# ReLU and row sum over 64 MB: own semaphores, multi-row instructions and a split memory layout

## Chip, cores, metric

The kernel runs on one core of one Trainium2 chip and uses no other. The metric is the device time of one execution in microseconds (us). Every run also has a traced span, from the first to the last instruction of the program. All runs quoted are marked fast in the record (none is more than 1.5% above the fastest of its kernel), with a granted clock of 1.0.

## The reference

```python
batch, seq, dim = 32, 512, 1024
x = np.random.randn(batch, seq, dim).astype(np.float32)

def reference(x):
    relu_x = np.maximum(x, 0)
    return np.sum(relu_x, axis=-1).astype(np.float32)
```

That is 16384 rows of 4 KB: 67.1 MB to read, 64 KB to write, hardly any arithmetic.

## The kernel before

Each of the 128 partitions owns 128 consecutive rows, so the 128 read streams of a load are 512 KB apart in memory. Seven loads of 16 rows per partition (8 MB each) go through two buffers; then come 8, 4, 2 and 1 rows and the last row in four pieces. Every row is one call that does ReLU and sum together (the profile shows two instructions for it, the second reads the accumulator), even rows on ScalarE and odd rows on VectorE.

```python
xv = x_flat.rearrange("(p m) d -> p (m d)", p=P)
out2d = out.rearrange("b s -> (b s)").rearrange("(p m) -> p m", p=P)
chunks = [16] * 7 + [8, 4, 2, 1]
io_pool = ctx.enter_context(tc.tile_pool(name="io", bufs=2))
...
for j, cpd in enumerate(chunks):
    xt = io_pool.tile([P, cpd, D], fp32, ...)
    nc.sync.dma_start(out=xt, in_=xv[:, m0 * D : (m0 + cpd) * D]...)
    for c in range(cpd):
        m = m0 + c
        if m == NT - 2:
            act_op(...)
            nc.scalar.dma_start(out=out2d[:, 0 : NT - 2], in_=res[:, 0 : NT - 2])
        elif (c % 2) == 0:
            act_op(xt[:, c, :], xt[:, c, :], m)       # ReLU with accumulated sum
        else:
            dve_op(xt[:, c, :], xt[:, c, :], res[:, m : m + 1])
    m0 += cpd
# last row in pieces of 244, 252, 260, 268 columns, all on VectorE; then:
nc.sync.dma_start(out=out2d[:, NT - 2 : NT], in_=res[:, NT - 2 : NT])
```

The first load is issued ahead of the program's opening barrier, in both kernels.

## Time and profile before

| | before |
|---|---|
| time, median (range) | 163.64 us (163.27 to 163.69), 3 runs |
| traced span | 161.5 us |
| load queue's packets, share of 16 engines | 96.9% |
| VectorE, ScalarE busy | 46%, 43% |

The page of the kernel before: the engines' busy time, the DMA queues (packets, MB, share of 16 engines), and the two costliest groups (busy us, mean ns of one | idle us before them, and what ended it):

```profile
DVE 74.3 (46%) x134; ACT 69.0 (43%) x129; POOL 0.2 (0%) x4
...
q1 hardware_dynamic: 2304, 67.11, 96.9%
q10 hardware_dynamic: 144, 0.06, 0.1%
q14 instruction: 2, 0.02, 0.0%
...
L79 DVE TENSOR_SCALAR_CACHE_REDUCE xt<-xt 128x1024 f32<-128x1024 f32 x63 | 72.6, 1216 | 84.5 <-DMA xt<-in_x_dram 84.2
L71 ACT ACTIVATE xt<-xt 128x1024 f32<-128x1024 f32 x64 | 66.7, 1043 | 89.0 <-DMA xt<-in_x_dram 89.0
```

Both compute engines are idle more than half of the time, waiting for loads. The line `q14` is easily passed over: two packets, together 16 KB, with which the engines' instruction streams are refilled, on the same 16 DMA engines as the loads.

The timeline of VectorE shows where each block of 16 rows has landed (start us, duration us, instruction, and in brackets the idle time before it; only the first instruction of a block is kept):

```profile
22.27 1.22 DVE L79 TENSOR_SCALAR_CACHE_REDUCE xt<-xt 128x1024 f32<-128x1024 f32 x1 [22.27 <-DMA xt<-in_x_dram]
...
61.08 1.22 DVE L79 TENSOR_SCALAR_CACHE_REDUCE xt<-xt 128x1024 f32<-128x1024 f32 x1 [10.27 <-DMA xt<-in_x_dram]
80.43 1.22 DVE L79 TENSOR_SCALAR_CACHE_REDUCE xt<-xt 128x1024 f32<-128x1024 f32 x1 [10.14 <-DMA xt<-in_x_dram]
100.27 1.22 DVE L79 TENSOR_SCALAR_CACHE_REDUCE xt<-xt 128x1024 f32<-128x1024 f32 x1 [10.63 <-DMA xt<-in_x_dram]
119.62 1.22 DVE L79 TENSOR_SCALAR_CACHE_REDUCE xt<-xt 128x1024 f32<-128x1024 f32 x1 [10.15 <-DMA xt<-in_x_dram]
```

The gaps are 19.35 us, but from 80.43 to 100.27 it is 19.84. The packet records and the landing events (semaphore updates by a DMA engine) in the trace say why. They are not a view of the page, so here they are in a plain fence:

```
instruction packets of 8192 bytes within the span: at 86.35 and 86.65 us, 309 ns each
last two of a block's 16 landing events:   block 3   80.20, 80.29 us
                                           block 4   99.63, 100.13 us
```

From block 4 on one engine is about half a microsecond behind the other fifteen, and a block has landed when its last engine has. The delay stays to the end. The ordinary 64 KB packet takes 2418 ns, so 16 engines carry 16 x 65536 B / 2.418 us = 433.7 GB/s. The Trainium skill's fabric ceiling is 435 GB/s ("DMA: Bandwidth & Descriptors", Where 436 GB/s comes from); the trace agrees. The same passage lets about 358 GB/s bind for loads from HBM; the loads of this one core run above that.

### The profile page before, as it was taken

The numbers are of one execution on the slowest core, as the hardware profiler recorded it, in microseconds if no ns is written. First come the engines' busy times: TensorE is split into PE (matmuls) and PEld (weight loads), VectorE is DVE, ScalarE is ACT, GpSimd is POOL, SyncE is SP. The second block draws the span as 40 slices with busy tenths as digits, with TensorE's granted clock in tenths as the row PEclk, the third lists the DMA queues.
The fourth block names the chain that finished last, engine by engine and source line by source line (L and its number), as shares of the span: only waits on it lengthen the run. The fifth ranks groups of instructions, "written<-read, shape, count | busy, mean of one in ns | idle before, by whom it ended". The sixth has DMA issues, their size and how long they took to land.

```text
span 161.5 us, 347 instructions
## 1 busy us (share of the span) xinstructions
DVE 74.3 (46%) x134; ACT 69.0 (43%) x129; POOL 0.2 (0%) x4
## 2 busy tenths in 40 slices
DVE  0000049700695008940099101991039900598983
ACT  3000049500693008920099001990039700596882
POOL 0000000000000000000000000000000000000000
DMA  8997997996997997997996997997997997999990
GB/s 308 471 503 308 487 487 308 503 503 292 503 503 308 487 503 325 471 519 308 471 519 296 487 503 325 471 503 341 454 503 341 454 503 308 430 438 406 406 359 22
DMA packets 2450, 67.19 MB, mean 416 GB/s; under 512 B 528, under 2 KB 1040, under 8 KB 1168
## 3 DMA queue, kind: packets, MB, share of 16 engines
q1 hardware_dynamic: 2304, 67.11, 96.9%
q10 hardware_dynamic: 144, 0.06, 0.1%
q14 instruction: 2, 0.02, 0.0%
HBM read 67.11 MB, written 0.07 MB: 416 GB/s over the span
## 4 chain that ended last, share of the span: by engine, by line
DMA 79%; DVE 18%; SPq 1%; issue 0%; DVEq 0%
DMA xt<-in_x_dram 62%; DVE xt L79 17%; DMA p<-in_x_dram 17%; SPq L95 1%; DVE p L79 1%; DVEq L79 0%; DVEq L16 0%
## 5 line engine op out<-in xcount | busy, mean ns | idle before, releaser
L79 DVE TENSOR_SCALAR_CACHE_REDUCE xt<-xt 128x1024 f32<-128x1024 f32 x63 | 72.6, 1216 | 84.5 <-DMA xt<-in_x_dram 84.2
L71 ACT ACTIVATE xt<-xt 128x1024 f32<-128x1024 f32 x64 | 66.7, 1043 | 89.0 <-DMA xt<-in_x_dram 89.0
L71 ACT ACTIVATION_READ_ACCUMULATOR xt<-xt 128x1 f32 x64 | 11.9, 187 | 0.0
L79 DVE DVE_READ_ACCUMULATOR xt<-xt 128x1 f32 x63 | 5.2, 83 | 0.0
L79 DVE TENSOR_SCALAR_CACHE_REDUCE p<-p 128x244 f32<-128x244 f32 (+3 forms) x4 | 1.6, 420 | 0.4 <-DMA p<-in_x_dram 0.4
L71 ACT ACT_TABLE_LOAD x1 | 1.3, 1283 | 0.8 <-PEq L143 0.8
L79 DVE DVE_READ_ACCUMULATOR p<-p 128x1 f32 x4 | 0.3, 82 | 0.0
L143 POOL MEMSET const-bfloat16-1.0<- 128x1 bf16 x1 | 0.1, 101 | 0.0
L143 POOL MEMSET const-uint8-127<- 128x1 uint8 x1 | 0.1, 101 | 0.0
L143 POOL MEMSET const-float32-0.0<- 128x1 f32 x1 | 0.1, 98 | 0.2 <-issue 0.2
L143 POOL MEMSET const-float32-1.0<- 128x1 f32 x1 | 0.1, 98 | 0.0
## 6 DMA issues: line engine op xcount, KB each, us to landing
xt<-in_x_dram SPq DMA_DIRECT2D x1, 4096.0 KB, 19.6
xt<-in_x_dram SPq DMA_DIRECT2D x1, 2048.0 KB, 24.2
xt<-in_x_dram SPq DMA_DIRECT2D x1, 1024.0 KB, 26.2
xt<-in_x_dram SPq DMA_DIRECT2D x1, 512.0 KB, 27.0
p<-in_x_dram SPq DMA_DIRECT2D x1, 134.0 KB, 10.0
p<-in_x_dram SPq DMA_DIRECT2D x1, 130.0 KB, 26.5
p<-in_x_dram SPq DMA_DIRECT2D x1, 126.0 KB, 26.7
p<-in_x_dram SPq DMA_DIRECT2D x1, 122.0 KB, 26.8
```

The costliest lines, as they stand in the source:

```text
L71: nc.scalar.activation(out=out_ap, in_=in_ap, func=mybir.ActivationFunctionType.Relu, accum_out=res[:, m : m + 1],)
L79: nc.vector.tensor_scalar(out=out_ap, in0=in_ap, scalar1=0.0, scalar2=None, op0=mybir.AluOpType.max, op1=mybir.AluOpType.add, accum_out=ac ...
L95: nc.sync.dma_start(out=xt, in_=xv[:, m0 * D : (m0 + cpd) * D].rearrange("p (c d) -> p c d", c=cpd),)
L143: nc = _bacc.Bacc("TRN2", target_bir_lowering=False, num_devices=1)
```

## The change

Its intent: semaphores of its own in place of the framework's (one per load, so that no issue waits for a semaphore's reuse); one ReLU over up to 16 rows on ScalarE and one sum over the same rows on VectorE, so far fewer instructions; three buffers, because the two steps take longer from end to end; the first 8 MB of memory as the first block (partitions 64 KB apart), the rest as a second region (448 KB apart); all stores on SyncE, one more because the output too is now in two regions. Cut to its core:

```diff
+ROWS = 16
+NBUF = 3
+TWO = [[16], [16], [16], [8, 8], [8, 8], [6, 5], []]   # rows per ReLU and per sum
+ACT = [0, 0, 0, 0, 0, 5, 8]                             # single rows, ScalarE
+DVE = [0, 0, 0, 0, 0, 0, 8]                             # single rows, VectorE
...
-    xv = x_flat.rearrange("(p m) d -> p (m d)", p=P)
+    N1 = P * ROWS
+    xf = x_flat[:N1].rearrange("(p m) d -> p m d", p=P)
+    xv = x_flat[N1:].rearrange("(p m) d -> p m d", p=P)
...
+    def clamp(ap, loaded):                # ReLU of n rows, in place
+        i = nc.scalar.activation(out=ap, in_=ap, func=RELU)
...
+    def total(ap, m, n):                  # their sums
+        nc.vector.tensor_reduce(
+            out=res[:, m : m + n], in_=ap, axis=mybir.AxisListType.X, op=ADD
+        ).wait_op(sems.act, n_act, "sem-ge").then_inc(sems.dve, 1)
...
+    for j in range(NB):
+        buf = bufs[j % NBUF]
+        loaded = load(buf[:, :, :], rows(m, ROWS), j >= NBUF and freed[j - NBUF])
...
+        for n in TWO[j]:
+            clamp(buf[:, c : c + n, :], act_waits)
+            total(buf[:, c : c + n, :], m + c, n)
...
-                nc.scalar.dma_start(out=out2d[:, 0 : NT - 2], in_=res[:, 0 : NT - 2])
+    store(0, ROWS, *freed[0])
+    store(ROWS, NT - ROWS - 2, n_act - 1, n_dve)
...
-    nc.sync.dma_start(out=out2d[:, NT - 2 : NT], in_=res[:, NT - 2 : NT])
+    store(NT - 2, 2, n_act, n_dve)
```

The tail loads (8, 4, 2, 1 rows and four pieces) keep their sizes and their single-row instructions.

## The prediction

> **What bounds it now.** The load queue. Block landings (the timeline, where VectorE resumes) come every 19.35 us: 22.27, 41.61, 61.08, 80.43, 100.27, 119.62, 138.97; one gap is 19.84. In the trace's packet records nearly all 896 packets of 64 KB take 2418 ns, 27.1 GB/s an engine, 433.7 over 16: the ceiling of 435 that the Trainium skill gives ("DMA: Bandwidth & Descriptors", Where 436 GB/s comes from), and this trace agrees. ScalarE and VectorE wait 89.0 and 84.2 us for loads (the groups); the next load always queues 10 us before the one under way ends, so two buffers never starve the queue.
>
> Outside the stream: first packets start between 1.02 and 2.27 us, engine after engine, and take 2.55 to 3.2 us instead of 2.42; the last piece lands at 158.60; VectorE ends 159.19, the store's issue starts 159.25, it lands 160.67, the program ends 161.52.
>
> **What the change does.**
> 1. Fewer instructions. At 86.35 us, when ScalarE and VectorE have each recorded about 64 instructions, two 8 KB instruction-fetch packets (309 ns each) run on a load engine; from the next block on, one engine lands 0.49 us behind the others (100.13 against 99.63), and keeps that to the end (158.60 against 158.12). By count from the code both engines now stay below 60, so the fetches should vanish: -0.5 us, on the path.
> 2. Layout. The skill (same page, Latency and other measured facts) has a 512 KiB row pitch at 207 GB/s against 214 padded, for copies between HBM tensors. Here the 512 KB pitch already streams at full rate, so a 448 KB pitch gains nothing in mid-stream. It may cure the slow first packets: the engine that starts last loses 0.13 us there, only that counts. A few packets near 11 us are slow too, on engines with slack. -0.1 us.
> 3. Three buffers and two-pass compute. Estimated from traced slopes (ACTIVATE 1043 ns a row with about 190 fixed; VectorE 435-407 ns for 271-244 elements): ReLU of 16 rows 13.9 us, sum 17.1 us, both below 19.35. A buffer frees about 31 us after landing and the load into it goes out about 8 us before the queue empties, so still no starvation. The two engines become much busier (VectorE from 74 to about 100 us), off the path. The split [8,8], [6,5]+5 lets VectorE catch up at about 138, when block 6 lands.
> 4. Own semaphores. Two waits and a drain after the final store's landing (160.69 to 160.85) become one: -0.1 us. The wait of the third piece's issue on a reused semaphore (16.4 us, the queue's waits) goes, but it was hidden.
> 5. A third store, 64 B per partition: it queues behind the last piece and lands before the final store. About 0. The last sums and the 1.4 us of the final store remain.
>
> **Sum.** -0.5 -0.1 -0.1: about -0.7 of 163.64.
>
> Predicted 162.9 us, 162.4 to 163.4. Chances: faster by over 2% 0.01, within 2% 0.97, slower 0.02. The stream alone takes 64 x 2.418 = 154.8 us an engine, so 2% (3.3 us) can't be found in what is left.
>
> **What would show it.** No instruction packets between 0 and the end; every landing gap 19.35 us; last piece at about 158.0; span about 160.8; ACTIVATE of 128x16384 near 13.8 us and the reduction near 17.1 us; each load issued about 8 us before its predecessor lands.
>
> **What would make it wrong.** The reduction running well below one element a cycle, so that buffers come free late and the load queue runs dry (slower by several us); the 448 KB pitch or multi-row accesses slowing the 2418 ns packets; an instruction fetch moved into the tail rather than removed; the HBM's slow first packets costing more than the last engine shows, which would gain more.

## The result

| | before | changed |
|---|---|---|
| time, median (range) | 163.50 us (163.27 to 163.69), 4 runs | 163.09 us (162.92 to 163.43), 4 runs |
| ratio, 95% interval | | 0.9978 (0.9956 to 1.0001) |
| traced span of the profiled run | 161.5 us | 160.7 us |
| measured time of that run | 163.31 us | 163.14 us |
| rest (time less span) | 1.8 us | 2.4 us |

This first interval still includes 1; that of the repeat below (changed_again) doesn't.

The time lies inside the predicted range, but the traced span fell by 0.8 us and the time by 0.4: about half of the traced gain does not arrive. First the profile after, the same parts of the page:

```profile
DVE 117.0 (73%) x47; ACT 102.8 (64%) x52; POOL 0.2 (0%) x4
...
q1 hardware_dynamic: 2592, 67.18, 97.6%
...
L119 DVE TENSOR_REDUCE res<-io 128x8 f32<-128x8192 f32 (+3 forms) x9 | 97.9, 10933 | 40.1 <-ACT io L111 40.1
L111 ACT ACTIVATE io<-io 128x8192 f32<-128x8192 f32 (+3 forms) x9 | 79.2, 8826 | 47.2 <-DMA io<-in_x_dram 47.2
```

VectorE went from 46% to 73% busy and the kernel became no slower: the extra work lies under the loads. The `q14` line is gone, and the packets' share of the engines rose from 96.9% to 97.6%. The timeline of ScalarE, where the blocks land now:

```profile
21.95 13.86 ACT L111 ACTIVATE io<-io 128x16384 f32<-128x16384 f32 x1 [19.88 <-DMA io<-in_x_dram]
41.29 13.86 ACT L111 ACTIVATE io<-io 128x16384 f32<-128x16384 f32 x1 [5.48 <-DMA io<-in_x_dram]
...
80.00 13.95 ACT L111 ACTIVATE io<-io 128x8192 f32<-128x8192 f32 x2 [5.50 <-DMA io<-in_x_dram]
99.34 13.95 ACT L111 ACTIVATE io<-io 128x8192 f32<-128x8192 f32 x2 [5.39 <-DMA io<-in_x_dram]
118.70 9.68 ACT L111 ACTIVATE io<-io 128x6144 f32<-128x6144 f32 x2 [5.41 <-DMA io<-in_x_dram]
```

The first block lands 0.3 us earlier, the gap from 80.00 to 99.34 is an ordinary 19.34, and ReLU over 16 rows takes 13.86 us. The Trainium skill gives 186 ns + 0.833 ns an element for an ACTIVATE with immediate scale and bias ("ScalarE: Activation LUTs", What ACT_TABLE_LOAD costs), by which I estimate 13.83 us for 16384 elements; the trace agrees.

The chain of work that ended last, by line (shares of the span), of the kernel before:

```profile
by line: DMA xt<-in_x_dram 61.9%; DVE xt L79 17.1%; DMA p<-in_x_dram 16.6%; SPq L95 1.1%; DVE p L79 1.0%; issue 0.4%; DVEq L79 0.1%; DVEq L16 0.0%
```

The same view of the changed kernel, with two of the chain's pieces in order of time (start us, us, what):

```profile
by line: DVE res L119 32.1%; DMA io<-in_x_dram 25.2%; DMA piece<-in_x_dram 17.9%; ACT io L111 17.3%; another core or an unknown queue 3.4%; SPq L93 1.0%; DVE piece L136 0.7%; DVE piece L204 0.3%; issue 0.2%; DVEq L29 0.0%
...
74.54 51.60 DVE res L119 x5
...
126.16 0.33 SPq L93
```

This view misleads here. Loads fell from 79% of the chain to 43%, as if VectorE were the limit. The chain goes through the wait of the tail's first load for its buffer, which VectorE frees at 126.14 us; but the block before it in the queue lands only at 138.06 us, so the engines had 12 us of queued work when that issue went out. A chain follows what released an issue, not what kept the queue full. That the landing gaps stayed at 19.35 us is the better evidence.

What the page cannot show lies behind the span. The packet record of the changed kernel has one more instruction packet:

```
changed kernel:  8192 bytes of instructions at 162.81 us, 568 ns;  span ends at 160.70 us
kernel before:   none behind the span (161.52 us)
```

So the theory to test: the instruction fetch was not removed but moved behind the program's end, and there it costs what it had cost in the stream. Rivals: the layout made the whole gain; or the rest grew for another reason, such as the number of semaphores, or by chance.

### The profile page after: what moved, and what is told of

It reads as the page before. It is cut to its first block, busy times and chain, and to the rows that moved or that the text cites. A ratio compares the mean times of both kernels' runs of the same rounds, so it can differ in the third digit from the quotient of the medians.

```text
span 160.7 us, 162 instructions
## 1 busy us (share of the span) xinstructions
DVE 117.0 (73%) x47; ACT 102.8 (64%) x52; POOL 0.2 (0%) x4
## 3 DMA queue, kind: packets, MB, share of 16 engines
q1 hardware_dynamic: 2592, 67.18, 97.6%
## 4 chain that ended last, share of the span: by engine, by line
DMA 43%; DVE 33%; ACT 17%; another core or an unknown queue 3%; SPq 1%; issue 0%; DVEq 0%
DVE res L119 32%; DMA io<-in_x_dram 25%; DMA piece<-in_x_dram 18%; ACT io L111 17%; SPq L93 1%; DVE piece L136 1%; DVE piece L204 0%; DVEq L29 0%
## 5 line engine op out<-in xcount | busy, mean ns | idle before, releaser
L119 DVE TENSOR_REDUCE res<-io 128x8 f32<-128x8192 f32 (+3 forms) x9 | 97.9, 10933 | 40.1 <-ACT io L111 40.1
L111 ACT ACTIVATE io<-io 128x8192 f32<-128x8192 f32 (+3 forms) x9 | 79.2, 8826 | 47.2 <-DMA io<-in_x_dram 47.2
L126 ACT ACTIVATE io<-io 128x1024 f32<-128x1024 f32 x21 | 21.9, 1044 | 6.8 <-DMA io<-in_x_dram 6.8
L136 DVE TENSOR_SCALAR_CACHE_REDUCE io<-io 128x1024 f32<-128x1024 f32 x15 | 17.4, 1215 | 0.9 <-DMA io<-in_x_dram 0.8
L126 ACT ACTIVATION_READ_ACCUMULATOR io<-io 128x1 f32 x21 | 3.9, 187 | 0.0
L136 DVE TENSOR_SCALAR_CACHE_REDUCE piece<-piece 128x244 f32<-128x244 f32 (+2 forms) x3 | 1.2, 416 | 0.4 <-DMA piece<-in_x_dram 0.4
L136 DVE DVE_READ_ACCUMULATOR io<-io 128x1 f32 x15 | 1.2, 82 | 0.0
```

What stands on the lines that cost most here:

```text
L111: i = nc.scalar.activation(out=ap, in_=ap, func=RELU)
L119: nc.vector.tensor_reduce(out=res[:, m : m + n], in_=ap, axis=mybir.AxisListType.X, op=ADD).wait_op(sems.act, n_act, "sem-ge").then_inc(se ...
L126: i = nc.scalar.activation(out=ap, in_=ap, func=RELU, accum_out=res[:, m : m + 1])
L136: i = nc.vector.tensor_scalar(out=ap, in0=ap, scalar1=0.0, scalar2=None, op0=MAX, op1=ADD, accum_out=accum_out,)
```

## The experiments

Each was built from one of the two kernels and run on one chip together with the kernel before. The changed kernel itself ran only in the first result and in changed_again, so comparisons with it go through the kernel before. All differences lie within 2%; what counts is which intervals leave out 1. Spans and rests are means over all runs of that label; the kernel before gives 161.6 to 161.7 and 1.78.

| run | median us | ratio to before (95%) | mean span | rest |
|---|---|---|---|---|
| changed (first result) | 163.09 | 0.9978 (0.9956 to 1.0001) | 160.77 | 2.36 |
| changed_again | 162.98 | 0.9974 (0.9959 to 0.9988) | 160.68 | 2.29 |
| same_again | 163.39 | 0.9992 (0.9978 to 1.0006) | 161.58 | 1.78 |
| layout_only | 163.15 | 0.9981 (0.9967 to 0.9994) | 161.37 | 1.77 |
| old_layout | 163.46 | 1.0002 (0.9989 to 1.0015) | 161.23 | 2.25 |
| single_rows | 163.15 | 0.9978 (0.9963 to 0.9993) | 161.30 | 1.79 |
| waits_after_last_row | 162.82 | 0.9964 (0.9943 to 0.9986) | 160.80 | 2.06 |
| waits_in_stream | 163.01 | 0.9973 (0.9955 to 0.9992) | 161.25 | 1.78 |
| fewer_scalar | 162.83 | 0.9971 (0.9943 to 0.9999) | 160.90 | 2.09 |
| fewer_both | 162.49 | 0.9941 (0.9924 to 0.9958) | 160.72 | 1.77 |
| contiguous_block_last | 163.29 | 0.9995 (0.9979 to 1.0011) | 160.93 | 2.40 |
| waits_on_both | 163.10 | 0.9983 (0.9968 to 0.9998) | 160.90 | 2.19 |
| shorter_vector | 162.34 | 0.9938 (0.9924 to 0.9951) | 160.72 | 1.76 |

### The kernel before against itself: same_again

No edit.

> The kernel before, submitted again as it is, to see its scatter and the difference between measured time and traced span over several runs. If the difference of 1.8 us (163.31 measured, 161.5 traced) belongs to the kernel, its runs all show about 1.8 us, where the changed kernel shows 2.3 to 2.4. If it is luck of one run, the runs scatter between 1.8 and 2.4. Time ratio to before 1.000 within 0.002; two instruction packets near 86 us again.

The ratio was 0.9992, and the rest was 1.78 us in the mean of its six runs and of the eleven control runs. The rest belongs to the kernel; it is no luck. The two instruction packets came again, at 86.53 and 86.78 us.

### The layout alone: layout_only

```diff
-    xv = x_flat.rearrange("(p m) d -> p (m d)", p=P)
-    out2d = out.rearrange("b s -> (b s)").rearrange("(p m) -> p m", p=P)
+    N1 = P * big
+    xf = x_flat[:N1].rearrange("(p m) d -> p (m d)", p=P)
+    xv = x_flat[N1:].rearrange("(p m) d -> p (m d)", p=P)
+    of, ov = ...                      # the output in the same two regions
...
+    nc.sync.dma_start(out=of, in_=res[:, 0:big])      # third store, after the pieces
```

> The kernel before with nothing but the new layout (first block at a pitch of 64 KB, the rest at 448 KB, a third store). Fetch theory: the 0.31 us by which the first block landed earlier (22.24 to 21.93) is mostly scatter of the start, so the time stays within 0.2 us of before, and the instruction packets near 86 us stay with their 0.5 us. Layout theory: the first block lands at 21.9 instead of 22.24 and the time falls by 0.3 us.

The mean time fell by 0.31 us (163.45 to 163.14) and the mean span by 0.30 (161.67 to 161.37). The instruction packets stayed, at 83.78 and 86.32 us. VectorE's first instruction in this run:

```profile
21.93 1.22 DVE L83 TENSOR_SCALAR_CACHE_REDUCE xt<-xt 128x1024 f32<-128x1024 f32 x1 [21.93 <-DMA xt<-in_x_dram]
```

It starts 0.34 us earlier than in the kernel before (22.27). Here the layout theory was right and mine, that this was scatter of the start, was wrong.

### The layout taken back: old_layout

```diff
-    xf = x_flat[:N1].rearrange("(p m) d -> p m d", p=P)
-    xv = x_flat[N1:].rearrange("(p m) d -> p m d", p=P)
+    xall = x_flat.rearrange("(p m) d -> p m d", p=P)
+    xf, xv = xall[:, :ROWS, :], xall[:, ROWS:, :]
```

(and the output likewise)

> The changed kernel with the old layout, a pitch of 512 KB everywhere (the three stores kept). Fetch theory: the changed kernel's time to 0.1 us (about 163.1), no instruction packet in the span, last piece at about 158.0. Layout theory: first block back at 22.2, every later landing 0.3 us later, time 0.3 us above the changed kernel.

The ratio went to 1.0002: without the layout the whole rest of the change is worth nothing in measured time, although the mean span (161.23) is 0.4 us under that of the kernel before. The first block landed late again:

```profile
22.40 13.86 ACT L111 ACTIVATE io<-io 128x16384 f32<-128x16384 f32 x1 [20.33 <-DMA io<-in_x_dram]
```

What differs inside the first block can be counted in the packet records. Leaving out the first packet of each engine, packets of block 0 that took over 100 ns more than 2418: 6 in the kernel before, 3 in same_again, 12 in old_layout; none in layout_only, in the changed kernel or in any later run with another layout. These packets do not set the landing, though: in all fourteen traces the block lands 17.25 to 17.29 us after the end of the latest first packet, whether slow packets follow or not (seven more packets of 2.418 us and about 0.3 us for the landing). The latest first packet ends at 4.98 to 5.14 us in the three traces with a pitch of 512 KB throughout, and at 4.45 to 4.69 us in the eleven others. So what the new layout gains is gained in the first packets. In later blocks the two layouts run alike, at landing gaps of about 19.35 us (up to 19.46 in old_layout).

### The multi-row instructions taken back: single_rows

```diff
-TWO = [[16], [16], [16], [8, 8], [8, 8], [6, 5], []]
-ACT = [0, 0, 0, 0, 0, 5, 8]
-DVE = [0, 0, 0, 0, 0, 0, 8]
+TWO = [[], [], [], [], [], [], []]
+ACT = [8, 8, 8, 8, 8, 8, 8]
+DVE = [8, 8, 8, 8, 8, 8, 8]
...
+            nc.sync.wait_ge(sems.act, after[0])   # a buffer is free when both are done
```

> The changed kernel with single-row instructions alone (8 rows on ScalarE and 8 on VectorE in each of the seven blocks), semaphores, three buffers and layout kept. Fetch theory: the two 8 KB instruction packets come back, in block 3 as in the kernel before (near 86 us), one engine falls 0.5 us behind and the span grows by about 0.5 us against the changed kernel; the measured time less the span goes back to 1.8 us if the larger rest of the changed kernel (2.4) is a fetch that only moved behind the span, so that the measured time hardly differs. Layout theory: time equal to the changed kernel's.

The time equals the changed kernel's (ratio 0.9978 for both), with a span 0.5 to 0.6 us longer (161.30 against 160.77 and 160.68) and a rest that is back at 1.79. The fetch is back among the page's queues:

```profile
q14 instruction: 2, 0.02, 0.0%
```

And one gap is long in ScalarE's timeline:

```profile
60.57 1.06 ACT L128 ACTIVATE io<-io 128x1024 f32<-128x1024 f32 x1 [10.92 <-DMA io<-in_x_dram]
80.89 1.06 ACT L128 ACTIVATE io<-io 128x1024 f32<-128x1024 f32 x1 [11.89 <-DMA io<-in_x_dram]
```

That is 20.32 us between landings instead of 19.35. The packets ran at 64.56 and 67.38 us, a block earlier than I had expected. So the multi-row instructions do shorten the stream by half a microsecond, and the time does not change.

### The fetch moved by hand: waits_after_last_row, waits_in_stream

The first adds, after ScalarE's last row:

```diff
+    for _ in range(12):
+        nc.scalar.wait_ge(sems.loads[0], 16)
```

> The changed kernel with twelve more instructions on ScalarE after its last row: waits on the first load's semaphore, long satisfied. Moved-fetch theory (the instruction fetch that left the stream comes back behind the span, at 162.8 us, and costs there what it saved): if ScalarE's count is what decides it, the fetch now starts near 158 us, behind the last load and under the last sums and the store; measured time less span falls from 2.4 to 1.8 us at a span of 160.7, so about 162.5 measured. Rival (the rest outside the span has another cause, such as the number of semaphores, or another engine fetches): the rest stays at 2.4 us and the time at 163.1.

The rest fell to 2.06 us, about half of the way to 1.78; the span stayed at 160.80, and the ratio was 0.9964. ScalarE's stream had grown by seven recorded instructions (twelve waits don't appear as twelve in the trace; the forty of the next run appear as twenty). The instruction packet now ran at 161.08 us instead of 162.81, not near 158 as I had expected, and half of the extra rest stayed. I took it that a second fetch was still behind; the trace records none after this packet.

The second adds, after the first instruction of both engines:

```diff
+        if j == 0:
+            for _ in range(40):
+                nc.scalar.wait_ge(sems.loads[0], 16)
+                nc.vector.wait_ge(sems.loads[0], 16)
```

> The changed kernel with forty satisfied waits more on each of ScalarE and VectorE, after their first instruction. Moved-fetch theory: both engines need their next 8 KB before the end of the stream; two instruction packets appear inside the span, an engine falls behind by up to 0.5 us if they fall to one that is among the last, the span grows to about 161.2 and the rest outside falls to 1.8 us; measured time about 163.0, as the changed kernel. Rival: span 160.7, rest 2.4 us.

All as the moved-fetch theory had it: two instruction packets inside the span (143.25 and 144.39 us), span 161.25, rest 1.78, time 163.01. The forty useless waits show no cost of their own in the time; the fetches moved.

### The fetch taken away: fewer_scalar, fewer_both

These give wrong results on purpose in a few columns.

```diff
+        if j == 5:                      # both runs: one ReLU for five rows, no sums
+            clamp(buf[:, c : c + 5, :], None)
...
+        if j == 6:                      # fewer_both only: one maximum for eight rows
+            nc.vector.tensor_scalar(out=buf[:, c : c + 8, :], ..., op0=MAX)
```

(The columns of the result that nobody writes are set to zero by GpSimd.)

> The changed kernel with nine instructions fewer on ScalarE: the five single rows of block 5 become one ReLU without a sum (wrong results in those five columns, on purpose). Moved-fetch theory, if the fetch behind the span is ScalarE's and comes because its 58 instructions are close to the limit: no packet behind the span, rest 1.8 us, time about 162.5. Rival: rest stays at 2.3 to 2.4 us and the time at 163.1.

> As the run before, and the eight single rows of VectorE in block 6 become one instruction without a sum (fifteen fewer; wrong results on purpose). Moved-fetch theory: rest outside the span 1.8 us, time about 162.5, if one of these two engines does the fetch behind the span. If the rest stays at 2.3 to 2.4 us here too, the number of their instructions is not what decides it in this range, and the fetch behind the span belongs to the end of every short program.

With ScalarE nine instructions shorter the rest was 2.09; with VectorE fifteen shorter too it was 1.77, at a span of 160.72. The mean time of fewer_both was 162.50 us, against 163.14 and 162.98 for the changed kernel, which does the same loads. No instruction packet was recorded from the span's start to the end of the trace in either of the two. So one part of the extra rest, 0.2 to 0.3 us, goes with ScalarE's stream and another, 0.3 us, with VectorE's, and both vanish when the streams are short enough. That each part is a fetch of that engine's own is inferred: the changed kernel's trace has one packet behind the span, not two. The number of semaphores, my rival, can't be it: there is even one more in these two runs, and the rest fell. (The profiled execution of fewer_scalar was an outlier, 163.60 us with a span of 161.5; its other three runs have 160.6 to 160.8.)

Whether a packet behind the span counts in the measured time can be read from the traces, which still record semaphore updates of the program's closing there (moments are counted from the span's start). In the seven profiled runs with a rest of about 1.78 the last update comes 1.90 us after the span, and the measured time is 0.12 us less than that update's moment. In the four runs where an instruction packet outlasts the last update (changed, changed_again, old_layout, contiguous_block_last) the measured time is 0.23 us less than the packet's end in every one, and 0.23 to 0.46 us more than the last update's moment. So there it is the late packet with which the measured time ends. In waits_after_last_row and fewer_scalar the measured time is 0.15 and 0.16 us more than the last update's moment with no packet recorded there; a second fetch that the trace missed would fit, but is not shown.

### Which pitch matters: contiguous_block_last, with changed_again as control

```diff
-    N1 = P * ROWS
+    M1 = NT - ROWS
+    N1 = P * M1              # 112 rows at 448 KB first, the contiguous 8 MB last
```

> The changed kernel again, as a control beside the two below. Span 160.8, rest outside the span 2.3 to 2.4 us, time about 163.1, ratio to before 0.998.

> The changed kernel with the contiguous 8 MB block at the end of memory instead of the beginning: the first block too is read at a pitch of 448 KB, the tail at 64 KB. Theory A (the power-of-two pitch of 512 KB makes packets of the first block slow, any other pitch cures it): no slow packets after the first of each engine in block 0, first block landed at 21.7 to 21.9, span and time as the changed kernel's (160.8, 163.1). Theory B (the first block must be contiguous, at 64 KB): slow packets as with the old layout (4 to 14 of them more than 0.1 us late), first block landed at 22.2 to 22.4, span 161.2, time 163.5.

The control did as expected (span 160.68, rest 2.29, ratio 0.9974). With the contiguous block last, the first block, read at 448 KB, had no slow packet and landed at 21.95 us, as in the changed kernel (21.93). What block 0 suffers from is the pitch of 512 KB, and it need not be contiguous. That is theory A but for its "power-of-two": the pitches of block 0 were 512, 448 and 64 KB, and the last is a power of two as well. But the time did not follow. It was 0.35 us above the control (means 163.33 and 162.98), 0.25 of that in the span and 0.11 in the rest. In the trace the last piece lands 0.11 us later than in the control's (157.88 against 157.77), and the final store takes 1.52 us from issue to landing instead of 1.40. But the changed kernel's first trace has its last piece at 157.89 too, and same_again a store of 1.53, so both are within what repeats of one kernel show. The difference stays open. The first block's landing is what the run settles, not the time.

### The way to a better version: waits_on_both, shorter_vector

```diff
+    for _ in range(12):
+        nc.scalar.wait_ge(sems.loads[0], 16)      # after ScalarE's last row
...
+    for _ in range(12):
+        nc.vector.wait_ge(sems.loads[0], 16)      # after VectorE's last sum
```

> The changed kernel with twelve satisfied waits at the end of ScalarE's work, which took 0.3 us off the rest outside the span, and twelve more at the end of VectorE's. If each of the two engines has a fetch of its own behind the span that costs 0.3 us, the rest falls to 1.8 us at a span of 160.8: about 162.5, ratio 0.994. If VectorE's part was not a fetch, the rest stays at 2.06 and the time at 162.85. If the longer streams push the fetch back into the loads, as with forty waits, span 161.2 and time 163.0.

This missed: rest 2.19 and time 163.10. Two packets were recorded, at 160.98 and 162.36 us, both behind the span's end at 160.69. Neither outlasted the program's closing: here the last semaphore update itself came late, 2.32 us after the span instead of 1.90, and the measured time is again 0.12 us less than its moment. So the loss sits between the span's end and that update, and which engine or fetch held it up the trace doesn't say. I can't tell beforehand how many waits would be enough.

So the last run made VectorE's stream shorter instead, with correct results. A single row costs two instructions (the sum and the read of the accumulator); three rows by one maximum and one sum cost two in all.

```diff
-ACT = [0, 0, 0, 0, 0, 5, 8]
-DVE = [0, 0, 0, 0, 0, 0, 8]
+ACT = [0, 0, 0, 0, 0, 5, 9]
+DVE = [0, 0, 0, 0, 0, 0, 4]
+DVE2 = [0, 0, 0, 0, 0, 0, 3]     # three rows: tensor_scalar max, then tensor_reduce
...
+        if n == 8:                # the load of 8 rows: five single on ScalarE,
+            ...                   # three by one maximum and one sum on VectorE
...
+    for _ in range(8):
+        nc.scalar.wait_ge(sems.loads[0], 16)
```

> A correct version with 12 instructions fewer on VectorE (three rows of block 6 and three of the 8-row load are done by one maximum and one sum over three rows; ScalarE takes one single row more in each) and eight satisfied waits at the end of ScalarE. If a shorter VectorE stream needs no fetch of its own behind the span, as when fifteen were dropped, and ScalarE's fetch starts near 161 us, as with twelve waits, the rest outside the span falls to 1.8 or 1.9 us at a span of 160.7 to 160.8: 162.5 to 162.6, ratio to before 0.995. If twelve are too few or the longer ScalarE stream fetches inside the loads, the rest stays at 2.1 to 2.4 or the span grows to 161.2, and the time is 163.0, as the changed kernel.

It is correct, and its median is 162.34 us: ratio to before 0.9938 (0.9924 to 0.9951), where the changed kernel's control has 0.9974 (0.9959 to 0.9988). The rest is 1.76 at a span of 160.72. It beats both kernels, by 0.6% and about 0.4%; the second figure compares different chips through the kernel before. In its profiled execution, one of the two slower ones (162.75 us), the page's queues have one instruction packet:

```profile
q14 instruction: 1, 0.01, 0.0%
```

It ran at 157.81 us, under the last piece, and the view of the waits (us in total, times, longest us) shows VectorE waiting for that piece:

```profile
DVE piece L233 <- DMA piece<-in_x_dram: 0.5, 1, 0.5
```

The changed kernel's VectorE has no wait for the last piece.

## Why the prediction was right, point by point

The time was predicted at 162.9 us, 162.4 to 163.4, and measured at 163.09. The bound was right: the 64 KB packets stayed at 2418 ns, the landings at 19.35 us, and half as much work again for the compute engines (VectorE 74.3 to 117.0 us, ScalarE 69.0 to 102.8) changed nothing. But the gain was put at 0.7 us and came to 0.4, and it lies in the range by luck: two of its terms erred in opposite directions.

1. "-0.5 us, on the path" for the fetches. The mechanism was right inside the span: the packets left it, the gap at block 4 is 19.34 us, and bringing them back (single_rows, waits_in_stream) made the span 0.5 to 0.6 us longer. The failed step is "the fetches should vanish". They came back behind the span (one packet is recorded there, a second is inferred), where the rest grew from 1.78 to about 2.3 us. The term's worth in measured time is about nothing: single_rows has the changed kernel's ratio, and old_layout that of the kernel before. The prediction named "an instruction fetch moved into the tail rather than removed" as a danger, but thought of the end of the loads and not of the time after the last instruction, which the profile's span doesn't cover.
2. "-0.1 us" for the layout was a third of its size. It measured 0.31 us alone (layout_only); taken back, it cost about 0.4 (ratio 1.0002 instead of 0.9974 or 0.9978). The failed step is "the engine that starts last loses 0.13 us there, only that counts". The first packets do decide when block 0 lands, and the slow ones near 11 us were on engines with slack, as predicted. But the engine that starts last (2.27 us) ends its first packet at 4.81; another starts at 1.87, takes 3.11 us for it and ends at 4.98. In the changed kernel the latest end is 4.68, and the block lands 0.31 us earlier. My list of dangers had it: first packets "costing more than the last engine shows, which would gain more". Why the pitch makes the first packets end late the runs don't show. The mid-stream part ("gains nothing in mid-stream") was right.
3. "So still no starvation" was right. ReLU over 16 rows took 13.86 us (13.9 predicted) and the sum 17.22 (17.1); the loads went out 7.5 to 11.9 us before their predecessors landed (about 8 predicted), and VectorE caught up at 138.0 us. (The "about 190 fixed" has no source in the trace before, where ACTIVATE has one size only; the changed trace gives 190 ns, from 1044 ns for 1024 elements and 13.86 us for 16384.)
4. Own semaphores, "-0.1 us": from the landing of the final store to the end of the span it is 0.85 us before (160.67 to 161.52) and 0.80 after (159.90 to 160.70), so 0.05. No run isolates more of it.
5. The third store, "about 0": no run isolates it, but layout_only has it too and gained as a whole.

So: predicted 0.5 + 0.1 + 0.1; measured about 0 + 0.3 + 0.05, which fits the 0.4 us between the medians.

## What to carry to other kernels

When a kernel is bound by one stream of transfers, everything that uses the same DMA engines counts, including instruction refills; but check that a cost that left the trace also left the measured time, by comparing time and span over several runs. An effect that only one part of a change can have is worth one run of that part alone: here the smallest-looking part, the pitch of the first block, made nearly the whole measured gain. And a half microsecond that had only been moved could be won after all, by changing the lengths of both instruction streams: in shorter_vector VectorE's is 12 recorded instructions shorter and ScalarE's 9 longer, in fewer_both (with wrong results) both are shorter.

## What the Trainium skill lacked or had wrong

- "Runtime: NRT & Kernel Launch", Instruction fetch mechanics, has refills in blocks of 16 KiB and calls their cost mostly hidden. The packets recorded here are 8 KB (whether two of them make one such block the traces don't say), 309 ns each beside the loads; two of them made a landing gap 0.49 us longer (before) or 0.97 us (single_rows). In four profiled runs a packet behind the program's end is what the measured time ends with, and the rest is 2.22 to 2.44 us there instead of 1.78. A kernel that lives on the load queue does see them.
- That section counts 256 instructions to a block but does not say at which instruction of a stream a refill comes. The packets ran when 60 to 66 instructions were recorded on ScalarE in the kernel before and in layout_only, at 42 to 48 in single_rows, at 53 to 55 in waits_in_stream, and not within the 58 of the changed kernel. These runs don't settle the rule.
- "DMA: Bandwidth & Descriptors", Latency and other measured facts, gives the loss from a 512 KiB pitch for copies between HBM tensors (207 GB/s, where 214 is called full). For loads into SBUF on one core it shows here in the first block alone, whose latest first packet ends at 4.98 to 5.14 us instead of 4.45 to 4.69, and costs about 0.3 us of 163; afterwards the packets run at 2418 ns at either pitch.
- No page that I read tells that the time behind the traced span, which the measured time has in it, can depend on the kernel's own instruction streams: 1.78 us of rest for the kernel before, about 2.3 for the changed one.
